# Where linear attention's outputs are gated, and when their gates are fetched, in a one-core hybrid layer

## The chip, the cores and the metric

The kernel runs on one core of a Trainium2 chip. The core has TensorE for matmuls (PE; its weight loads, PEld, overlap them), VectorE (DVE), ScalarE (ACT), GpSimd (POOL) and SyncE (SP); each works through its own instructions in order, and 16 transfer engines move data between memory and SBUF for the queues of SP, ACT and POOL. Matmuls accumulate in PSUM banks of 128 x 512 fp32. The metric is device time in microseconds (us) of one execution.

## The reference

One layer, 256 tokens, width 2048, fp32. From x come three groups of dilated attention (8 heads of 128), a gated linear attention (4 heads, 512 values each) and gates:

```
parts = split(x @ w_in)                       # 9 attention parts, gq, gk, gv, gr, g_low, m_a, m_b
ya = softmax-weighted sum of the 3 groups' outputs @ w_proj_a
o  = linear attention(gq, gk, gv, decay from g_low), per head
o  = o * rsqrt(mean(o * o) + eps) * gla_norm_g
yb = (o * silu(gr)) @ w_proj_b
y  = sigmoid(m_a) * ya + sigmoid(m_b) * yb
x  = layernorm(alpha * x + y @ w_out)
x  = layernorm(alpha * x + (silu(conv3(x @ w_gate)) * (x @ w_up)) @ w_down)
```

silu(gr) is gr * sigmoid(gr). What is called *gating* below is o * silu(gr), for each head h and each half t of the tokens (128 tokens x 512 values).

## The kernel before

Each fp32 weight piece (128 x 1024, 512 KB) is loaded by SP and split into two parts that PE multiplies at full rate: ACT copies the high part (`whi`, L137), DVE subtracts for the low part (`wlo`, L138). There are six buffers for high parts and four for low ones. PE then takes three matmuls for one product (high x high, low x high, high x low). So every weight passes ACT and DVE before PE, and what stands ahead of a split in ACT's or DVE's order delays it.

The stages, in PE's order:

- **First stage** (to about 838 us): tiles of q and k (`b16`, L237) alternate with units of seven products (`seven`, L318) for the values `v`, the linear attention's `gv`, `gr`, and the gates `m`. Their results are spilled to memory. Beside them run short steps: attention's (list `side`) and linear attention's (list `slow`: for each head fetch, decay, keys, scores, outputs, the last spilling o by L723). `pump` (L186) is called between steps; it takes one step of `slow` on every second call and one or more of `side` on each. A step may carry a mark and waits until the unit that passes this mark is done.
- **Plain gate chunks** (L788, 838 to 889 us; tiles `m_t`): the last quarter of the gates by plain products (`a_chunk`, L268). The projected attention outputs are fetched and split meanwhile (`ya_parts`, L780).
- Then the pool of early buffers is closed and one of late buffers is opened at the same place in SBUF (L796, L797). The first instruction that uses the late pool is POOL's memset of three buffers (L801).
- **yp** (L859): four chunks of ya @ w_proj_a. Each chunk fetches its two gates from memory on POOL's queue, takes their sigmoid (L855), and multiplies them with the product (L863). Beside yp run the four steps `gated_out` (L837): fetch gr and o of a head into the late pool, sigmoid (L843), two products (L844, L845), and turn the result by PE into PSUM banks (`transposed`, L805 and L814), from which ACT and DVE take its high and low part (L821, L822) as the operand `ob` of the next stage.
- **pb** (L869): four chunks of the gated outputs @ w_proj_b, times their gates, plus ya. Then w_out, the layer norm, and the feed-forward part (from 1135 us), which the change leaves alone.

ACT loads a table of functions when an instruction needs one that isn't loaded (`ACT_TABLE_LOAD`): exponential and logarithm stand in one, sigmoid in another.

The order on each engine is set by a scheduler that places the recorded instructions, so that it differs from the order of the code; buffers and the recorded dependences bound it.

Of the kernel before, what the change touches and what calls it, by code (L numbers as in the profile page):

```python
# [11 lines left out]
F32 = mybir.dt.float32  # L12
F32R = mybir.dt.float32r
AF = mybir.ActivationFunctionType
# [3 lines left out]
P = 128  # L18
S = 256
# [39 lines left out]
def hybrid_layer(ctx: ExitStack, tc: tile.TileContext, wp, xt, wgl, gw, par, relb, onehot, rows, xk, out):  # L59
# [53 lines left out]
    def fetch(name, d, make=None, by=None):  # L113
        b = (make or blk)(name)
        (by or nc.gpsimd).dma_start(b, d)
        return b
# [19 lines left out]
    def split(hi, lo, src):  # L136
        nc.scalar.activation(hi, src, AF.Copy)  # L137
        nc.vector.tensor_tensor(lo, src, hi.bitcast(F32), op=ALU.subtract)  # L138
# [485 lines left out]
    def gla(h):  # L624
# [153 lines left out]
    YA2 = [res("ya") for _ in range(2)]  # L778

    def ya_parts(h):  # L780
        def f():
            y = YA2[h // 4][:, h % 4]
            split(y[:, :S], y[:, S:], fetch("yaf", YA[h], tmp))
        return f

    side.extend(ya_parts(h) for h in range(NH))
    yop = lambda kc: YA2[kc // 4][:, kc % 4]
    for n in range(2):  # L788
        pss = a_chunk("m", xop, 16, AT["mb"] + 8 * n, 3)
        for t in range(2):  # L790
            c = blk("mc")
            nc.scalar.activation(c, pss[t], AF.Copy)
            M[1][2 + n][t] = spill("ms", c)
    drain()
    home[:] = "quarter", 12
    early.close()  # L796
    now[:] = ctx.enter_context(tc.tile_pool(name="late", bufs=1)), (17, 10, 1)  # L797
    gbufs = []
    for i in range(3):
        g = now[0].tile([P, S + 2], F32, name=f"gbuf{i}")  # L800
        nc.gpsimd.memset(g[:, 0:2], 0.0)  # L801
        gbufs.append(g)


    def transposed(name, n, halves_of_tokens, gain=None):  # L805

# [25 lines left out]
        return opnd  # L832


    OB = []

    def gated_out(h):  # L837
        def f():
            g = []
            for t in range(2):  # L840
                x, o = fetch("gr", GR[h][t]), fetch("o", O[h][t])
                sg = blk("sg")
                nc.scalar.activation(sg, x, AF.Sigmoid)  # L843
                nc.vector.tensor_tensor(sg, sg, x, op=ALU.mult)  # L844
                nc.vector.tensor_tensor(sg, sg, o, op=ALU.mult)  # L845
                g.append(sg)
            OB.extend(transposed("ob", h, g, P_NG))
        return f

    side.extend(gated_out(h) for h in range(GH))  # L850
    last_gate = []

    def gate(br, n, t):
        g = fetch("m", M[br][n][t])
        last_gate[:] = [nc.scalar.activation(g, g, AF.Sigmoid)]  # L855
        return g

    ya = []
    for n in range(4):  # L859
        g = [gate(0, n, t) for t in range(2)]  # L860
        pss = a_chunk("yp", yop, 8, AT["pa"] + 4 * n)
        for t in range(2):
            nc.vector.tensor_tensor(g[t], g[t], pss[t], op=ALU.mult)  # L863
        ya.append(g)
    drain()


    YT = []
    for n in range(4):  # L869
        g = [gate(1, n, t) for t in range(2)]  # L870
        pss = a_chunk("pb", by_pairs(OB), 16, AT["pb"] + 8 * n)
        for t in range(2):
            y = g[t]
            nc.vector.tensor_tensor(y, y, pss[t], op=ALU.mult)
            nc.vector.tensor_tensor(y, y, ya[n][t], op=ALU.add)
        side.append(lambda n=n, y=g: YT.extend(transposed("yt", n, y)))
    drain()

# [272 lines left out]
```

## Time and profile before

| | us |
|---|---|
| median of three runs (1877.98 to 1884.69) | 1882.73 |
| the profiled execution's own time | 1883.29 |
| its span, first to last instruction | 1881.6 |
| PE / DVE / ACT / POOL busy | 1835.3 / 1348.2 / 1037.2 / 153.1 |
| first stage and plain gate chunks end, yp begins | 889.15 |
| yp ends, pb begins | 945.93 |

The profile is of one execution. A row of a timeline reads: start, duration, engine, line, operation, written<-read tiles, shapes, and in brackets how long the engine was idle before and what ended that. A row of waits reads: engine, tile and line that waited, what it waited for; sum in us, times, longest. A row of windows: the stretch, its length, busy us and instructions of PE, PEld, DVE, ACT and POOL, the granted share of TensorE's clock, the busy share of the transfer engines, GB/s. A group's row ends with busy us, mean ns of one | idle us before them and what ended it.

### The profile page before, as it was taken

The page shows a single profiled execution, that of the slowest core. Times are in us where ns is not written, and L with a number is a line of the kernel's source. Part 1 is how long each engine was busy: PE and PEld are TensorE (multiplying, and loading weights), DVE is VectorE, ACT ScalarE, POOL GpSimd, SP SyncE. Part 2 cuts the span into 40 slices and gives each one's busy share as a digit, 9 for nine tenths or more (in the row PEclk, how much of TensorE's full clock was granted, in tenths as well). Part 3 has the DMA queues.
Part 4 walks back from the last instruction along what each step waited for, and adds up shares of the span by engine and source line. Part 5 has one row for each costly group of instructions (what it writes and reads, how often), then busy time and mean ns, then how long its engine had stood idle before and what let it go on. Part 6 is the DMA issues. An engine that isn't in the chain of part 4 may idle for free.

```text
span 1881.6 us, 25449 instructions
## 1 busy us (share of the span) xinstructions
PE 1835.3 (98%) x9270; PEld 1549.8 (82%) x9270; DVE 1348.2 (72%) x1613; ACT 1037.2 (55%) x1346; POOL 153.1 (8%) x241
## 2 busy tenths in 40 slices
PE   8999999999999999999899999999999999999997
PEld 6778778888888888888688877888888888888885
DVE  7889878888787978875755568666546666456667
ACT  6467556666766666654644446555335554345452
POOL 0011111101111111101300001000000000000001
PEclk9999999999999999999999999999999999999998
DMA  8478996978979798795876557555655566565651
GB/s 313 166 282 255 305 319 184 341 223 270 325 224 343 203 307 287 244 333 179 313 235 204 196 168 232 188 193 187 201 185 195 182 196 194 192 231 193 193 167 45
DMA packets 131849, 432.39 MB, mean 230 GB/s; under 512 B 15601, under 2 KB 25868, under 8 KB 131724
## 3 DMA queue, kind: packets, MB, share of 16 engines
q1 hardware_dynamic: 96764, 345.09, 52.5%
q0 software_dynamic: 21424, 73.53, 15.9%
q10 hardware_dynamic: 13536, 12.16, 2.1%
q8 instruction: 72, 1.18, 0.2%
q14 instruction: 53, 0.43, 0.1%
HBM read 372.97 MB, written 21.14 MB: 209 GB/s over the span
## 4 chain that ended last, share of the span: by engine, by line
PE 86%; DMA 4%; DVE 2%; issue 1%; ACT 1%; DVEq 0%; SPq 0%; ACTq 0%; POOLq 0%
PE qk L228 9%; PE fu L228 8%; PE fg L228 8%; PE fu L230 4%; PE qk L230 4%; PE fg L230 4%; PE wd_t L264 4%; PE wd_t L266 4%; PE wd_t L265 4%; DMA quarter<-in_wp 2%; PE pb_t L266 2%; PE pb_t L265 2%; PE pb_t L264 2%; PE wo_t L264 2%; PE wo_t L265 2%; PE wo_t L266 1%
## 5 line engine op out<-in xcount | busy, mean ns | idle before, releaser
L138 DVE TENSOR_TENSOR wlo<-quarter,whi 128x1024 fp32r<-128x1024 f32 x624 | 747.6, 1221 | 354.2 <-PE wd_t L265 84.2
L137 ACT ACTIVATE whi<-quarter 128x1024 fp32r<-128x1024 f32 x624 | 655.8, 1057 | 478.6 <-PE wd_t L266 95.9
L137 ACT ACTIVATE whi<-raw 128x1024 fp32r<-128x1024 f32 (+1 forms) x146 | 151.4, 1044 | 86.4 <-PE qk L228 38.1
L228 PE MATMUL qk<-x,whi 128*128 128x512 f32 x768 | 195.2, 403 | 0.0
L138 DVE TENSOR_TENSOR wlo<-raw,whi 128x1024 fp32r<-128x1024 f32 (+1 forms) x146 | 173.3, 1205 | 30.6 <-ACT whi L137 10.8
L228 PEld LDWEIGHTS qk<-x,whi 128*128 128x128 f32 x768 | 143.6, 190 | 30.5 <-issue 1.2
L228 PE MATMUL fu<-x,whi 128*128 128x512 f32 x688 | 164.1, 391 | 0.0
L228 PE MATMUL fg<-x,whi 128*128 128x512 f32 x672 | 160.2, 390 | 0.0
L228 PEld LDWEIGHTS fu<-x,whi 128*128 128x128 f32 x688 | 126.4, 188 | 24.5
L228 PEld LDWEIGHTS fg<-x,whi 128*128 128x128 f32 x672 | 123.7, 188 | 24.0
L264 PE MATMUL wd_t<-whi,h 128*128 128x512 f32 x352 | 137.0, 389 | 0.0
L265 PE MATMUL wd_t<-wlo,h 128*128 128x512 f32 x352 | 137.0, 389 | 0.0
L266 PE MATMUL wd_t<-whi,h 128*128 128x512 f32 x352 | 136.9, 389 | 0.0
L345 DVE TENSOR_TENSOR quarter<-quarter,quarter 128x1024 f32<-128x1024 f32 x88 | 104.4, 1217 | 0.4
L230 PEld LDWEIGHTS qk<-x,wlo 128*128 128x128 f32 x768 | 98.6, 191 | 3.8
L230 PE MATMUL qk<-x,wlo 128*128 128x256 f32 x768 | 99.6, 283 | 0.0
L230 PEld LDWEIGHTS fu<-x,wlo 128*128 128x128 f32 x688 | 88.2, 191 | 3.4
L230 PE MATMUL fu<-x,wlo 128*128 128x256 f32 x688 | 89.2, 283 | 0.0
L348 POOL DMA_DIRECT2D quarter<-quarter x72 | 62.9, 873 | 321.7 <-DMA quarter<-in_wp 175.0
L230 PEld LDWEIGHTS fg<-x,wlo 128*128 128x128 f32 x672 | 86.2, 191 | 3.3
L230 PE MATMUL fg<-x,wlo 128*128 128x256 f32 x672 | 87.2, 283 | 0.0
L266 PEld LDWEIGHTS wd_t<-whi,h 128*128 128x128 f32 x352 | 66.1, 188 | 13.8
(316 smaller groups left out, 2765.7 us busy)
## 6 DMA issues: line engine op xcount, KB each, us to landing
quarter<-in_wp SPq DMA_DIRECT2D x504, 512.0 KB, 4.5
raw<-in_wp SPq DMA_DIRECT2D x142, 512.0 KB, 6.7
quarter<-quarter POOLq DMA_DIRECT2D x72, 512.0 KB, 9.5
row<-in_rows POOLq DMA_DIRECT2D x16, 256.0 KB, 5.1
sp<-c POOLq DMA_DIRECT2D x14, 256.0 KB, 9.2
bias<-bvd ACTq DMA_DIRECT2D x32, 96.0 KB, 5.4
v<-vs ACTq DMA_DIRECT2D x24, 128.0 KB, 4.5
m<-sp POOLq DMA_DIRECT2D x12, 256.0 KB, 4.8
```

The costliest lines, as they stand in the source:

```text
L137: nc.scalar.activation(hi, src, AF.Copy)
L138: nc.vector.tensor_tensor(lo, src, hi.bitcast(F32), op=ALU.subtract)
L228: nc.tensor.matmul(ps, parts(kc)[0], opnd(kc), start=(kc == 0), stop=False)
L230: nc.tensor.matmul(ps[:, S:], parts(kc)[1], opnd(kc)[:, :S], start=False, stop=(kc == nk - 1))
L264: nc.tensor.matmul(ps, xh, hi, start=first, stop=False)
L265: nc.tensor.matmul(ps, xh, lo, start=False, stop=False)
L266: nc.tensor.matmul(ps, xl, hi, start=False, stop=last)
L345: tt(a, a, b, op=ALU.add)
L348: nc.gpsimd.dma_start(a, b, accum_op=ALU.add)
```

## The change

Fetching gr and o, sigmoid and both products leave yp and become steps of `slow` in the first stage, behind linear attention's own steps and behind the mark "gr"; once that mark is passed, `pump` takes a step of `slow` on every call. The fetches go out on ACT's queue; the result is spilled (`og`) by POOL. The turned operands of heads 0 and 1 are made in the plain gate chunks, those of heads 2 and 3 in yp; each turn's operand is fetched in an earlier step. Fetch and split of the attention outputs are two steps now, the last two heads' in yp. The gates of yp and pb are fetched one chunk ahead, and their sigmoid is recorded behind the chunk's matmuls.

```diff
     def pump(n=1):
         turns[0] += 1
-        if turns[0] % 2 == 0:
+        if turns[0] % 2 == 0 or "gr" in passed:
             following(slow)
...
+    def gated(h):
+        st = []
+        def get():
+            for t in range(2):
+                st.append([fetch("gr", GR[h][t], by=nc.scalar), fetch("o", O[h][t], by=nc.scalar)])
+        def mul():
+            sgs = [blk("sg") for _ in range(2)]
+            for sg, (x, o) in zip(sgs, st):
+                nc.scalar.activation(sg, x, AF.Sigmoid)
+                nc.vector.tensor_tensor(x, x, o, op=ALU.mult)
+            for t, (sg, (x, o)) in enumerate(zip(sgs, st)):
+                nc.vector.tensor_tensor(sg, sg, x, op=ALU.mult)
+                O[h][t] = spill("og", sg)
+        return get, mul
...
         for stages in gla_stages:
             slow.extend(stages)
+        for h in range(GH):
+            get, mul = gated(h)
+            slow.extend([("gr", get), lambda: None, mul])
...
-        yield from by_unit("gr", 2, lambda u: to(GR, u))
+        yield from by_unit("gr", 2, lambda u: to(GR, u), "gr")
...
-    side.extend(ya_parts(h) for h in range(NH))
+    def ob_get(h):
+        def f():
+            got[h] = [fetch("og", O[h][t]) for t in range(2)]
+        return f
+    def ob_turn(h):
+        def f():
+            OB[2 * h : 2 * h + 2] = transposed("ob", h, got[h], P_NG)
+        return f
...
+    slow.extend([
+        lambda: (ob_get(0)(), ya_get(0, 1)),
+        lambda: ya_get(2, 3),
+        lambda: (ya_split(0, 1), ob_turn(0)()),
+        lambda: (ya_split(2, 3), ob_get(1)()),
+        lambda: ya_get(4, 5),
+        lambda: ob_turn(1)(),
+        lambda: ya_split(4, 5),
+    ])
     for n in range(2):
         pss = a_chunk("m", xop, 16, AT["mb"] + 8 * n, 3)
...
-    side.extend(gated_out(h) for h in range(GH))
+    def gates_ahead():
+        ahead = None
+        for br in range(2):
+            for n in range(4):
+                new = [fetch("m", M[br][n][t]) for t in range(2)]
+                if ahead is None and not (br or n):
+                    ya_get(6, 7)
+                    for h in (2, 3):
+                        ob_get(h)()
+                else:
+                    yield ahead
+                ahead = new
+        yield ahead
+    ahead_of = gates_ahead()
+    def gated_by(g, pss):
+        for x in g:
+            last_gate[:] = [nc.scalar.activation(x, x, AF.Sigmoid)]
+        for x, ps in zip(g, pss):
+            nc.vector.tensor_tensor(x, x, ps, op=ALU.mult)
+    side.extend([lambda: ya_split(6, 7), ob_turn(2), lambda: None, ob_turn(3)])
     for n in range(4):
-        g = [gate(0, n, t) for t in range(2)]
+        g = next(ahead_of)
         pss = a_chunk("yp", yop, 8, AT["pa"] + 4 * n)
-        for t in range(2):
-            nc.vector.tensor_tensor(g[t], g[t], pss[t], op=ALU.mult)
+        gated_by(g, pss)
```

(pb changes in the same way; `transposed` itself stays as it is.)

Three places in the engines' orders. The first is PE in yp, where it changes from chunk 0 (`yp_t_1069`/`1070` before, `yp_t_1117`/`1118` now) to chunk 1 (`yp_t_1095`; now `yp_t_1128`/`1129`). `pt` are the turns, read from a head's gated output (`sg` before, `og` now). Before:

```order
L264 MATMUL yp_t_1070_8162<-whi_8254,ya_7727 128x512
L265 MATMUL yp_t_1070_8162<-wlo_8255,ya_7727 128x512
L266 MATMUL yp_t_1070_8162<-whi_8254,ya_7727 128x512
L264 MATMUL yp_t_1095_8313<-whi_8317,ya_7726 128x512
L814 MATMUL pt_8216<-ident,sg_8203 128x128
L814 MATMUL pt_8225<-ident,sg_8203 128x128
L265 MATMUL yp_t_1095_8313<-wlo_8318,ya_7726 128x512
```

Now:

```order
L264 MATMUL yp_t_1118_8294<-whi_8355,ya_7807 128x512
L265 MATMUL yp_t_1118_8294<-wlo_8356,ya_7807 128x512
L266 MATMUL yp_t_1118_8294<-whi_8355,ya_7807 128x512
L807 MATMUL pt_8372<-ident,og_8281 128x128
L807 MATMUL pt_8372<-ident,og_8283 128x128
...
L807 MATMUL pt_8381<-ident,og_8283 128x128
L264 MATMUL yp_t_1129_8399<-whi_8402,ya_7806 128x512
```

Before, the turn of head 0 stood behind the 48 matmuls of chunk 0 and one of chunk 1; now that of head 2 stands behind the 48 and three of chunk 1, both halves together.

The second place is POOL's queue where the late pool opens: `ms` are the spills of the last plain gate chunk, `m` the gates of yp's first chunk. Before:

```order
L110 DMA ms_8119<-mc_8117 128x512
L110 DMA ms_8123<-mc_8121 128x512
L801 MEMSET gbuf_8149 128x2
...
L115 DMA m_8155<-sp_6111 128x512
L115 DMA m_8158<-sp_6234 128x512
L115 DMA gr_8199<-sp_4591 128x512
L115 DMA o_8201<-os_4305 128x512
L115 DMA gr_8207<-sp_4691 128x512
L115 DMA o_8209<-os_4317 128x512
```

Now:

```order
L110 DMA ms_8257<-mc_8255 128x512
L110 DMA ms_8261<-mc_8259 128x512
L878 MEMSET gbuf_8267 128x2
...
L115 DMA m_8273<-sp_6161 128x512
L115 DMA m_8275<-sp_6279 128x512
L115 DMA yaf_8277<-yas_7860 128x256
L115 DMA yaf_8279<-yas_8217 128x256
L115 DMA og_8281<-og_6849 128x512
L115 DMA og_8283<-og_6852 128x512
```

The two gates still come first behind the memset; the place of gr and o of head 0 is taken by two attention outputs of half the size and then the gated outputs of head 2.

The third place is the first stage. On DVE, before the first split (`wlo`) of the product `mB` of the second gate unit (`quarter` are the unit's weights, which are added to each other), there stood before:

```order
L658 TENSOR_TENSOR gz_6467<-gc_6236 128x512
L345 TENSOR_TENSOR quarter_6303<-quarter_6303,quarter_6474 128x1024
L345 TENSOR_TENSOR quarter_6305<-quarter_6305,quarter_6476 128x1024
L138 TENSOR_TENSOR wlo_6488<-quarter_6299,whi_6487 128x1024
```

Now (rows between left out):

```order
L740 TENSOR_TENSOR gr_6355<-gr_6355,o_6357 128x512
L740 TENSOR_TENSOR gr_6359<-gr_6359,o_6361 128x512
L742 TENSOR_TENSOR sg_6473<-sg_6473,gr_6355 128x512
L742 TENSOR_TENSOR sg_6474<-sg_6474,gr_6359 128x512
...
L345 TENSOR_TENSOR quarter_6375<-quarter_6375,quarter_6559 128x1024
L138 TENSOR_TENSOR wlo_6571<-quarter_6369,whi_6570 128x1024
```

The four products of head 0 have come in, one operation (L658) of the last linear attention head has gone to an earlier place. On ACT, some 25 us later, where an attention head's two exponentials stand (L476), before:

```order
L476 ACTIVATE s_825_6403,l_6650<-s_825_6403,nm_6648 128x384
L476 ACTIVATE s_826_6404,l_6657<-s_826_6404,nm_6655 128x768
L137 ACTIVATE whi_6730<-quarter_6474 128x1024
L137 ACTIVATE whi_6740<-quarter_6476 128x1024
L137 ACTIVATE whi_6765<-raw_6763 128x1024
```

Now, from the second of these exponentials on; ahead of it, between the two, stand a table load, the two sigmoids of head 1, and ahead of the first a further table load:

```order
L476 ACT_TABLE_LOAD
L476 ACTIVATE s_854_6486,l_6746<-s_854_6486,nm_6744 128x768
L137 ACTIVATE whi_6809<-quarter_6555 128x1024
L137 ACTIVATE whi_6819<-quarter_6557 128x1024
L115 DMA gr_6729<-sp_5355 128x512
...
L115 DMA o_6735<-os_5798 128x512
L256 ACTIVATE pa_6796<-qk_6763 128x256
L137 ACTIVATE whi_6829<-quarter_6559 128x1024
L739 ACT_TABLE_LOAD
L739 ACTIVATE sg_6842<-gr_6729 128x512
L739 ACTIVATE sg_6843<-gr_6733 128x512
L137 ACTIVATE whi_6866<-raw_6864 128x1024
```

The fetches of head 2 and its sigmoids have come between the splits, with one copy (`pa`) and one split between fetch and use. In all ACT's order holds eleven table loads where it held five.

More of the change, by code (lines that the diff above doesn't have):

```diff
@@ L775, in hybrid_layer @@
             done += 1
[L778 to L784, printed above, removed]
-    side.extend(ya_parts(h) for h in range(NH))
-    yop = lambda kc: YA2[kc // 4][:, kc % 4]
-    for n in range(2):
-        pss = a_chunk("m", xop, 16, AT["mb"] + 8 * n, 3)
-        for t in range(2):
[L791 to L802, printed above, removed]
     def transposed(name, n, halves_of_tokens, gain=None):
@@ L832, in by_pairs @@
         return opnd
-    OB = []
-    def gated_out(h):
+    OB = [None] * 8
+    got = {}
+    def ob_get(h):
         def f():
[L839 to L847, printed above, removed]
-        return f
@@ L850, in hybrid_layer, with ya_get @@
-    side.extend(gated_out(h) for h in range(GH))
-    last_gate = []
[L853 to L856, printed above, removed]
+            got[h] = [fetch("og", O[h][t]) for t in range(2)]
+        return f
+    def ob_turn(h):
+        def f():
+            OB[2 * h : 2 * h + 2] = transposed("ob", h, got[h], P_NG)
+        return f
+    YA2 = [res("ya") for _ in range(2)]
+    yaf = {}
+    def ya_get(*hs):
+        for h in hs:
+            yaf[h] = fetch("yaf", YA[h], tmp)
@@ new lines, in ya_split @@
+    def ya_split(*hs):
+        for h in hs:
+            y = YA2[h // 4][:, h % 4]
+            split(y[:, :S], y[:, S:], yaf[h])
+    slow.extend([
[7 more added lines that the diff above has]
+    ])
+    yop = lambda kc: YA2[kc // 4][:, kc % 4]
+    for n in range(2):
+        pss = a_chunk("m", xop, 16, AT["mb"] + 8 * n, 3)
+        for t in range(2):
+            c = blk("mc")
+            nc.scalar.activation(c, pss[t], AF.Copy)
+            M[1][2 + n][t] = spill("ms", c)
@@ new lines, in hybrid_layer @@
+    drain()
+    home[:] = "quarter", 12
+    early.close()
+    now[:] = ctx.enter_context(tc.tile_pool(name="late", bufs=1)), (17, 10, 1)
+    gbufs = []
+    for i in range(3):
+        g = now[0].tile([P, S + 2], F32, name=f"gbuf{i}")
+        nc.gpsimd.memset(g[:, 0:2], 0.0)
+        gbufs.append(g)
+    last_gate = []
+    def gates_ahead():
[11 more added lines that the diff above has]
+        yield ahead
```

8 lines of the change are left out of this document (3 added, 5 removed).

## The prediction

> **What bounds the kernel.** The page first: share of the engines, then the chain that ended last.
>
> ```profile
> PE 1835.3 (98%) x9270; PEld 1549.8 (82%) x9270; DVE 1348.2 (72%) x1613; ACT 1037.2 (55%) x1346; POOL 153.1 (8%) x241
> PE 86%; DMA 4%; DVE 2%; issue 1%; ACT 1%; DVEq 0%; SPq 0%; ACTq 0%; POOLq 0%
> ```
>
> TensorE is busy for 98% of the span and carries 86% of the chain. Whatever the change moves between the other engines is worth only what TensorE stops waiting, and it leaves TensorE's own work alone: the 32 turns of gated outputs stand elsewhere in its order, but none is added. So the second view is the list of waits, for PE.
>
> ```profile
> PE pt L814 <- issue: 7.7, 1, 7.7
> ...
> PE ps L465 <- DVE s L467: 4.2, 3, 2.9
> ```
>
> The longest wait of the whole execution is one of 7.7 us before a turn (L814), in the chunks that this change rewrites. The third view is PE's timeline around it, with the granted clock of the stretches behind it and of one after the 2.9 us wait of the second row.
>
> ```profile
> 900.03 0.39 PE L264 MATMUL yp_t<-whi,ya 128*128 128x512 f32 x1
> 908.14 0.66 PE L814 MATMUL pt<-ident,sg 128*128 128x128 f32 x2 [7.72 <-issue]
> 908.45 0.78 PE L265 MATMUL yp_t<-wlo,ya 128*128 128x512 f32 x1
> ...
> 911.57 0.39 PE L266 MATMUL yp_t<-whi,ya 128*128 128x512 f32 x1
> ```
>
> ```profile
> 281.00:286.80 5.80, 5.80 (x14) 4.56 (x15) 3.55 (x8) 3.55 (x7) 0.48 (x1) 0.50 0.97 391
> ...
> 904.80:908.10 3.30, 0.00 (x0) 0.00 (x0) 1.45 (x3) 2.48 (x4) 2.09 (x4) 0.50 1.03 417
> 908.20:911.40 3.20, 3.20 (x9) 2.62 (x10) 2.77 (x4) 0.80 (x2) 0.61 (x2) 0.50 1.01 408
> ```
>
> PE stops at 900.4 and takes up work at 908.14; the clock is at half from about 904.8 to 911.4, so the 3.1 us from 908.45 to 911.57 do 1.6 us of work. Wait and clock cost 7.7 + 1.5 = 9.2 us, 0.5% of the span. That is all there is to win here. The 2.9 us wait was followed by about 6 us at half clock too: a shorter wait starts again earlier inside the slow stretch and pays more of it.
>
> **What the wait consists of.** The timelines of PE, ACT and POOL, and four transfers, the two spills and two of the fetches (size, then us from issue to landing):
>
> ```profile
> 889.15 0.39 PE L264 MATMUL yp_t<-whi,ya 128*128 128x512 f32 x1
> ```
>
> ```profile
> 888.89 1.07 ACT L137 ACTIVATE ya<-yaf 128x256 fp32r<-128x256 f32 x3 [1.15 <-DMA yaf<-yas]
> 889.87 0.58 ACT L792 ACTIVATE mc<-m_t 128x512 f32<-128x512 f32 x1
> ...
> 890.65 0.59 ACT L792 ACTIVATE mc<-m_t 128x512 f32<-128x512 f32 x1
> ...
> 902.36 1.28 ACT L855 ACT_TABLE_LOAD   x1 [6.16 <-issue]
> ```
>
> ```profile
> 891.54 0.54 POOL L110 DMA_DIRECT2D ms<-mc  x1 [0.25 <-ACT mc L792]
> 896.90 0.17 POOL L801 MEMSET gbuf<- 128x2 f32 x3 [4.82 <-DMA quarter<-in_wp]
> 897.41 0.54 POOL L115 DMA_DIRECT2D m<-sp  x1 [0.34 <-issue]
> ...
> 899.73 0.54 POOL L115 DMA_DIRECT2D gr<-sp  x1
> ```
>
> ```profile
> ms<-mc POOLq DMA_DIRECT2D x1, 256.0 KB, 3.5
> ```
>
> ```profile
> ms<-mc POOLq DMA_DIRECT2D x1, 256.0 KB, 5.1
> ```
>
> ```profile
> m<-sp POOLq DMA_DIRECT2D x1, 256.0 KB, 4.7
> ```
>
> ```profile
> gr<-sp POOLq DMA_DIRECT2D x1, 256.0 KB, 7.3
> ```
>
> Let E be the end of the plain gate chunks, 889.15, where the first matmul of yp starts. Both results are copied out (to 891.2), the second spill goes out at 891.54 and lands 5.1 us later at 896.6 (the first spill took 3.5); only then is the early pool closed, and the memset at 896.90 opens the late one (the row's named releaser had long been done; the spill is what ends there). Every fetch into the late pool stands behind that: the first lands at 897.41 + 4.7, and only then ACT loads the sigmoid's table. PE has 49 matmuls of yp (11.1 us) to do meanwhile, and then stands at a turn.
>
> **The change there.** By the order of the changed kernel PE has 51 matmuls of yp, 51 x 0.227 = 11.6 us, and then the turn of head 2. Sigmoid, two products and the table load no longer stand ahead of that turn, but the gated output that it turns is again fetched into the late pool, as the fifth and sixth transfer after the same memset. So the barrier stays and only what followed it shrinks. In times from E: the three splits ahead of the first copy are gone, so the second copy ends at about E+1.1 to 1.4 (E+2.1 before); spill 3.5 to 5.1; memset and first issue E+5.5 to E+7.2 (E+8.3 before). The fifth transfer of 256 KB landed at 899.73 + 7.3 = 907.0, 9.6 us after the first issue; the two transfers of 128 KB among the six now make sixth place about equal to it: 9.6 to 10.3. The turn's operands are there at E+15.1 to E+17.5, against PE's arrival at E+11.6: a wait of 3.5 to 5.9 us, say 4.6. It begins as before, so the half clock begins as before too, and PE comes back with 4.5 to 6 us of it to run, which costs some 2.6 us. Together 7.2 against 9.2: a gain of **2.0 us**. Its ends: nothing, if the landings are as late as the latest above; and with the shortest of each (copies 1.1, spill 3.5, issue of six 3.2, landing 4.7) a wait of 0.9 us and no slow clock, a gain of 8.
>
> **What the change adds to the first stage.** The gating of four heads now lies between about 687 and 750 us: 16 fetches on ACT's queue, 8 sigmoids, 16 products on DVE, 8 spills, and six more table loads (the order shows eleven where there were five), because sigmoids now stand between exponentials. Prices and the state of that stretch (a window; then DVE, PE; fetches of the same size on ACT's queue; ACT, PE; groups):
>
> ```profile
> 700.00:710.00 10.00, 10.00 (x47) 8.31 (x46) 10.00 (x12) 8.06 (x10) 0.00 (x0) 1.00 0.07 16
> ```
>
> ```profile
> 703.48 4.62 DVE L138 TENSOR_TENSOR wlo<-quarter,whi 128x1024 fp32r<-128x1024 f32 x4
> ```
>
> ```profile
> 705.18 0.62 PE L332 MATMUL mB<-wlo,comb 128*128 128x512 f32 x2
> ```
>
> ```profile
> gq<-gkqs ACTq DMA_DIRECT2D x8, 256.0 KB, 8.3
> gv<-sp ACTq DMA_DIRECT2D x8, 256.0 KB, 10.8
> ...
> gc<-gcs ACTq DMA_DIRECT2D x4, 256.0 KB, 6.7
> ```
>
> ```profile
> 719.40 0.33 ACTq L453 DMA_DIRECT2D bias<-bvd  x1
> ...
> 724.21 1.06 ACT L137 ACTIVATE whi<-raw 128x1024 fp32r<-128x1024 f32 x1 [0.55 <-ACT whi L137]
> ```
>
> ```profile
> 733.40 3.91 PE L228 MATMUL qk<-x,whi 128*128 128x512 f32 x16
> ```
>
> ```profile
> L972 ACT ACT_TABLE_LOAD x1 | 1.3, 1283 | 0.0
> ```
>
> ```profile
> L843 ACT ACTIVATE sg<-gr 128x512 f32<-128x512 f32 x8 | 5.0, 624 | 0.8 <-DMA gr<-sp 0.8
> ```
>
> ```profile
> L844 DVE TENSOR_TENSOR sg<-sg,gr 128x512 f32<-128x512 f32 x8 | 5.5, 688 | 8.1 <-ACT sg L843 8.1
> ```
>
> *Head 0, on DVE.* DVE has no free time from 700 to 710, and the first of four splits at 703.48 ends at 704.7, when PE takes it at 705.18: half a microsecond to spare. In the new order head 0's four products (4 x 0.69 = 2.75 us) stand ahead of that split, and one operation of 0.68 us of the linear attention's last head has gone from there. Without any wait PE loses 2.75 - 0.68 - 0.5 = 1.6 us. The products also wait for the sigmoid, and that for its fetch, issued two splits and a copy out of PSUM before it, by PE's pace there an estimated 6 us; with the 8.3 us of the fetch rows about 1.2 us more, with 10.8 some 4 more, with 6.7 none. I take 2.4 (1.6 to 5.6).
>
> *Head 2, on ACT.* The order has the four fetches, one copy and one split, then table load and sigmoids: the fetch is used some 4 us after its issue and takes 6.7 to 10.8, so ACT stands still for about 4 us, and the splits of the following weights stand behind it. The piece next in line was made at 725.3 and taken at 733.40, 8.1 us to spare. Ahead of it come four table loads (5.1), four sigmoids (2.5), four issues (1.3) and that wait (4): 13 us, less an estimated 2 us in which ACT idled there (0.55 in its row) and the 2.4 that PE has already lost: 8.5 to 9 us. I take 2.0, more than the 0.5 left over, because DVE stands behind ACT; bounds 0 and 5 (with 10.8 us of landing). Heads 1 and 3 have their fetch long done by then, and I cost them at nothing; whi buffers six pieces ahead are their cover.
>
> [...]
>
> **The plain gate chunks.** Heads 0 and 1 are turned there; 16 of the 32 turns leave yp, which is PE's time moved and not changed. Their two banks are wanted again after 10 and 11 matmuls (2.3 and 2.5 us) by the last attention head, while four evictions on ACT, each followed by one on DVE, empty them:
>
> ```profile
> L821 ACT ACTIVATE ob<-pt,prm 128x256 fp32r<-128x256 f32 x16 | 6.8, 468 | 1.7 <-PE pt L814 1.4 <-DVE ob L822 0.3
> ```
>
> Four times 0.47 with a DVE step behind is 2.4 us, more if a split lies between. I take **0.8 us** (0 to 3). Gates fetched a chunk ahead I cost at nothing: their sigmoids already ran far ahead of need, hidden under yp's 44 us of matmuls; without that cover each pair would cost its 1.2 us.
>
> **The sum.** The profiled execution took 1883.29 us, 0.56 above the median of 1882.73, inside the spread of the three runs. 1883.29 - 2.0 + 2.4 + 2.0 + 0.8 = **1886.5 us**, 0.2% above the median.
>
> **Rivals.** *The wait goes.* If six transfers land within 5 us of the memset, PE meets its operands on time: minus 8, and with 1.6 us lost on DVE 1876.9. For it: the first landing of 4.7. Against: the fifth's 9.6 after the first issue, with the transfer engines full (1.03 and 1.01 in the two windows of the slow clock). 8%. *ACT blocked in the first stage.* Slower: where a fetch on ACT's queue takes 10 us or more, ACT's queue stands at the sigmoid of heads 0 and 2 until the weights run out; 5.6 + 5 us, and as each wait is then longer than the 2.9 after which the clock was seen at half, about 3 us more for one of them: 1883.3 - 2 + 10.6 + 3 + 0.8 = 1895.7; from about 9 us of landing it is over the bound of 0.3%. For it: the 10.8 us row. Against: the 6.7 us row. 36%, which includes the cases between the forecast and that price. *The change does nothing there*, since the first stage has room for all of it: 1883.3 - 2 = 1881.3; against it stands DVE's full window. This counts within the forecast's case, no difference.
>
> **Chances.** About 0.3%, 5.6 us, is what a measurement of this kernel tells from no change. No difference (the forecast and the last rival) 56%, slower by more 36%, faster by more 8%. Range: from 1878 (most of the wait gone, little lost) to 1895 (most of the second rival).
>
> **What would show it.** In the changed kernel's waits: a wait of PE at the turn of head 2, 3.5 to 5.9 us, about 11.6 us behind the start of yp, with half clock behind it; idle time of ACT before the new table loads; PE waiting for a split of DVE near 705 and for ACT or DVE near 735; a short wait of PE for a bank in the plain gate chunks. The forecast is wrong if the wait at the turn is under 1 us, or if the first stage's PE waits sum to under 1 or over 9 us.

## The result, and the profile after

The changed kernel took 1904.23 us in the median of six runs (1899.46 to 1910.25), where the kernel before, run beside it, took 1883.04 (1877.98 to 1885.63). The ratio is 1.0113 with a 95% interval of 1.009 to 1.0136: it is about 1.1% slower. The forecast was 1886.5 us with a range of 1878 to 1895, so the time lies outside the range, on the side of the rival *ACT blocked in the first stage*. The profiled execution took 1899.46 us.

The page of the changed kernel gives the share of the engines; PE does the same work as before (1835.3 us then) in a longer span:

```profile
PE 1836.0 (97%) x9270; PEld 1548.5 (82%) x9270; DVE 1347.8 (71%) x1613; ACT 1041.8 (55%) x1352; POOL 154.0 (8%) x241
```

The first matmul of each stage, in PE's timeline, cuts the two profiled executions into stretches (us):

| stretch | before | after | difference |
|---|---|---|---|
| first stage up to the gate units (`mA`) | 603.8 | 599.6 | -4.2 |
| gate units and attention, up to `m_t` | 234.8 | 254.4 | **+19.6** |
| plain gate chunks, up to `yp_t` | 50.6 | 57.2 | **+6.6** (1.8 of it the 16 turns that moved here) |
| yp, up to `pb_t` | 56.8 | 51.3 | **-5.4** (1.8 of it the turns that left) |
| all behind it | 935.7 | 935.3 | -0.4 |

The first row is not the change. Three kernels below leave the first stage as it was before, and the stretch from the first `v` unit to the first `gv` unit, which holds this difference, took 242.6, 244.5 and 244.9 us in them, 244.3 in the changed kernel, and 248.4 only in the one profiled execution of before. Without the turns that merely moved, the change costs 19.6 + 4.8 - 3.6 = 20.8 us.

PE's waits in the changed kernel (engine, tile and line, releaser: sum, times, longest) name the three places:

```profile
PE qk L228 <- ACT whi L137: 11.1, 3, 8.2
PE ps L465 <- DVE s L467: 8.8, 5, 2.6
...
PE yp_t L264 <- ACT ya L137: 4.1, 1, 4.1
```

**The gate units.** The longest wait of before, 7.7 us at a turn in yp, is gone, and one of 8.2 us stands in the first stage: PE waits for a high part that ACT makes. The timelines of PE and of ACT there show why (ACTq are the transfers that ACT issues):

```profile
736.93 0.27 PE L486 MATMUL ppt<-ident,s 128*128 128x128 f32 x1
...
745.44 0.80 PE L228 MATMUL qk<-x,whi 128*128 128x512 f32 x1 [8.23 <-ACT whi L137]
```

```profile
726.15 0.34 ACTq L115 DMA_DIRECT2D gr<-sp  x1
...
727.47 1.30 ACTq L115 DMA_DIRECT2D gr<-sp  x1
...
734.97 1.28 ACT L739 ACT_TABLE_LOAD   x1 [2.30 <-DMA gr<-sp]
736.26 0.63 ACT L739 ACTIVATE sg<-gr 128x512 f32<-128x512 f32 x1
743.81 0.63 ACT L739 ACTIVATE sg<-gr 128x512 f32<-128x512 f32 x1 [6.91 <-DMA gr<-sp]
744.34 1.99 ACT L137 ACTIVATE whi<-raw 128x1024 fp32r<-128x1024 f32 x2
```

The second `gr` of head 2 is issued at 727.47 and used at 743.81, 16.3 us later. ACT stands 2.3 us ahead of the table load and 6.9 ahead of the second sigmoid, and the split that PE needs at 737 is the next instruction on ACT's queue, at 744.34. Some 2.7 us into the wait, which begins at 737.2, the granted clock falls to 0.50. Windows of the changed kernel (stretch, length, busy us of PE, PEld, DVE, ACT and POOL, granted clock, share of the transfer engines, GB/s):

```profile
737.00:739.90 2.90, 0.20 (x2) 0.00 (x0) 0.44 (x1) 0.00 (x0) 0.00 (x0) 1.00 1.05 289
739.90:750.20 10.30, 4.76 (x11) 3.80 (x12) 3.59 (x6) 6.39 (x8) 1.62 (x3) 0.50 0.88 333
```

Of the 10.3 us at half clock 4.8 lie behind the wait, and cost 2.4 us of work: 8.2 + 2.4 = 10.6 us from this one place. DVE stood for the other operand of the gating too, 18 us in five waits:

```profile
DVE gr L740 <- DMA o<-os: 18.0, 5, 6.7
```

Transfers on POOL's queue were slow too, and they had been before. First the transfers issued between 725 and 745 us in the profile of *before* (size, us to landing), then those of the changed kernel:

```profile
sp<-c POOLq DMA_DIRECT2D x1, 256.0 KB, 13.0
sp<-s POOLq DMA_DIRECT2D x1, 256.0 KB, 8.5
bias<-bvd ACTq DMA_DIRECT2D x2, 96.0 KB, 10.7
```

```profile
og<-sg POOLq DMA_DIRECT2D x2, 256.0 KB, 17.1
sp<-c POOLq DMA_DIRECT2D x1, 256.0 KB, 18.2
```

So the trace of before held a part of the answer: in just this stretch 96 KB on ACT's queue took 10.7 us, and of two transfers of 256 KB on POOL's queue one took 13.0 and one 8.5. Why the second `gr` took 16.3 is not shown.

**The plain gate chunks.** ACT, DVE and PE of the changed kernel, around the second wait of the list (2.3 us of it here):

```profile
865.78 1.06 ACT L137 ACTIVATE whi<-raw 128x1024 fp32r<-128x1024 f32 x1 [1.60 <-DMA raw<-in_wp]
869.16 0.42 ACT L137 ACTIVATE ya<-yaf 128x256 fp32r<-128x256 f32 x1 [2.32 <-DMA yaf<-yas]
...
869.49 1.04 ACT L137 ACTIVATE whi<-raw 128x1024 fp32r<-128x1024 f32 x1
```

```profile
869.61 0.42 DVE L138 TENSOR_TENSOR ya<-yaf,ya 128x256 fp32r<-128x256 f32 x1 [3.40 <-ACT ya L137]
869.96 1.22 DVE L138 TENSOR_TENSOR wlo<-raw,whi 128x1024 fp32r<-128x1024 f32 x1
871.09 0.28 DVE L467 SCALAR_TENSOR_TENSOR s<-ps,bias 128x128 f32<-128x128 f32 x1
```

```profile
871.43 0.70 PE L465 MATMUL ps<-qk 128*128 128x256 f32 x2 [2.26 <-DVE s L467]
```

The split of an attention output waits 2.3 us for its fetch; DVE stands for it, a weight split is next, and only then comes the step that frees a bank of the attention head's scores. It is the same pattern as above. PE's waits in this stretch sum to 4.1 us: this one, one of 1.0 for a turn's bank and one of 0.8 for a copy of ACT; before the change it had none.

**yp.** POOL and PE of the changed kernel:

```profile
911.49 1.22 POOL L110 DMA_DIRECT2D ms<-mc  x2 [4.49 <-ACT mc L869]
917.27 0.17 POOL L878 MEMSET gbuf<- 128x2 f32 x3 [4.56 <-DMA ms<-mc]
...
918.85 1.06 POOL L115 DMA_DIRECT2D yaf<-yas  x2
```

```profile
919.69 0.39 PE L266 MATMUL yp_t<-whi,ya 128*128 128x512 f32 x1
924.22 0.80 PE L264 MATMUL yp_t<-whi,ya 128*128 128x512 f32 x1 [4.14 <-ACT ya L137]
```

The barrier of the two pools is as forecast: last spill, memset, then fetches. But PE does not stop at the turn of head 2. It stops sooner, inside chunk 0, whose last pieces read the attention outputs of heads 6 and 7, which the change now fetches into the late pool too.

### The profile page after: what moved, and what is told of

Its sections match the earlier page's. It is cut to its first block, busy times and chain, and to the rows that moved or that the text cites. A ratio compares the mean times of both kernels' runs of the same rounds, so it can differ in the third digit from the quotient of the medians.

```text
span 1897.7 us, 25455 instructions
## 1 busy us (share of the span) xinstructions
PE 1836.0 (97%) x9270; PEld 1548.5 (82%) x9270; DVE 1347.8 (71%) x1613; ACT 1041.8 (55%) x1352; POOL 154.0 (8%) x241
## 4 chain that ended last, share of the span: by engine, by line
PE 51%; issue 3%; DVE 1%; DMA 1%; ACT 1%; POOL 0%; POOLq 0%; DVEq 0%; ACTq 0%
PE fu L228 8%; PE fg L228 8%; PE fu L230 4%; PE fg L230 4%; PE wd_t L264 4%; PE wd_t L266 4%; PE wd_t L265 4%; PE wo_t L265 2%; PE wo_t L264 2%; PE pb_t L266 2%; PE pb_t L265 2%; PE pb_t L264 2%; PE wo_t L266 2%; PE yp_t L264 1%; PE yp_t L265 1%
```

## The experiments

Each kernel's one profiled execution was cut into the same stretches; ratios are against the kernel before, run beside it. In the expectations "from the second gate's units to the plain gate chunks" means the stretch from `mA` to `m_t`.

| kernel | `mA` to `m_t` | `m_t` to yp | yp | ratio, 95% interval |
|---|---|---|---|---|
| before | 234.8 | 50.6 | 56.8 | 1 |
| the changed kernel | 254.4 | 57.2 | 51.3 | 1.0113 (1.009 to 1.0136) |
| fetch farther ahead, all heads | 242.8 | 59.8 | 52.5 | 1.0078 (1.0061 to 1.0096) |
| the same, head 2 alone | 244.0 | 58.9 | 51.6 | 1.0063 (1.0038 to 1.0088) |
| fetch farther ahead, on POOL's queue | 241.0 | 62.0 | 52.3 | 1.0047 (1.0032 to 1.0062) |
| no fetches | 241.6 | 57.2 | 52.5 | 1.0041 (1.0025 to 1.0056) |
| fetches alone | 238.8 | 57.8 | 51.5 | 1.0057 (1.0035 to 1.008) |
| copy in place of sigmoid | 250.1 | 58.0 | 51.4 | 1.0098 (1.0065 to 1.0132) |
| gating alone moved | 254.4 | 50.5 | 57.6 | 1.0094 (1.0069 to 1.0118) |
| turns back in yp | 252.3 | 57.6 | 53.4 | 1.011 (1.0071 to 1.0148) |
| attention outputs early | 252.2 | 58.1 | 53.6 | 1.0124 (1.0106 to 1.0143) |
| before, turns late | 235.0 | 50.5 | 54.1 | 0.9994 (0.998 to 1.0008) |
| before, turns spread | 234.9 | 50.6 | 48.1 | 1.0011 (1.0 to 1.0022) |
| before, turns spread and gates ahead | 235.1 | 50.6 | 47.1 | 0.9966 (0.9952 to 0.9981) |

### Which part of the change carries the loss: the gating alone

The kernel before, with `gated`, its steps and `pump`'s new condition taken over, and `gated_out` cut to a fetch and the turns:

```diff
     def gated_out(h):
         def f():
-            g = []
...
+            g = [fetch("og", O[h][t]) for t in range(2)]
             OB.extend(transposed("ob", h, g, P_NG))
```

> The kernel before, with the gating alone moved into the first stage; turns, attention outputs and gates stay where they were, and the turns in yp read the fetched gated outputs. Theory (the first stage carries the loss): the stretch from the start of the second gate's units to the plain gate chunks is 17 to 21 us longer than before, the plain gate chunks stay within 1 us of before, the wait before the first turn in yp falls from 7.7 us to 3 to 5 us: 1894 to 1900 in all. Rival (the turns in the plain gate chunks and the fetch of attention outputs carry it): at most 6 us over the time before.

The stretch of the gate units is as long as in the whole change (254.4), and the plain gate chunks are as before (50.5). So the moved gating carries the 19.6 us, and nothing of the 6.6. The time, 1900.4 us, was just above the band expected, because one point of the theory missed: the wait before the first turn did not shorten.

```profile
924.17 0.66 PE L835 MATMUL pt<-ident,og 128*128 128x128 f32 x2 [8.45 <-DMA quarter<-in_wp]
```

It grew from 7.7 to 8.4 us, though sigmoid and products no longer stand ahead of the turn. (The releaser named is a weight's transfer; the turn reads `og`, whose fetches POOL issued from 917.4 on, behind its memset at 915.8.) What PE waited for in yp was the barrier and the landings, not the gating.

### Is it the landing: the fetch farther ahead

In the changed kernel:

```diff
-            slow.extend([("gr", get), lambda: None, mul])
+            slow.extend([("gr", get), *[lambda: None] * 4, mul])
```

> The changed kernel with one edit: three more idle steps between a head's fetch and its sigmoid, so that 13 to 25 instructions of ScalarE lie between the fetch of heads 0 to 2 and its use, where 4 to 20 lay. Table loads (11), sigmoids and products stay. Theory (ScalarE stands still at a sigmoid whose fetch hasn't landed, with the weights' splits behind it): ScalarE's idle time ahead of the gating's sigmoids and table loads (2.3 + 6.9 us at head 2) goes, the 8.2 us wait of TensorE before the qk tile and the 10.2 us at half clock behind it go too, and the time falls by 10 to 14 us, to 1886 to 1890. Rival (it is ScalarE's and VectorE's added work and the table loads, not the landing): the waits move with the work, and the time stays within 4 us of the changed kernel's.

The 8.2 us wait is gone, no idle time of ACT stands ahead of a gating sigmoid or its table load, and the stretch is 11.6 us shorter. The time was 1895.73 us, 8.5 below the changed kernel's, short of the 10 to 14 expected, as the plain gate chunks took back 2.6. And ACT still stood 7.2 us once, in another way:

```profile
756.06 0.33 ACTq L115 DMA_DIRECT2D gr<-sp  x1
...
757.28 0.33 ACTq L115 DMA_DIRECT2D o<-os  x1
...
759.36 0.33 ACTq L115 DMA_DIRECT2D gr<-sp  x1
...
762.32 0.33 ACTq L115 DMA_DIRECT2D o<-os  x1
...
762.75 2.01 ACT L137 ACTIVATE whi<-raw 128x1024 fp32r<-128x1024 f32 x2 [7.16 <-DMA gr<-sp]
```

Four issues of 0.33 us are 1.2 to 3 us apart, and the next split comes behind the last: here ACT stands at the *issue* of a fetch, which itself waits for an earlier transfer (which one is seen in the kernel with the fetches alone, below).

With the further idle steps for head 2 alone (`(4 if h == 2 else 1)`):

> The changed kernel with the three further idle steps between fetch and sigmoid for head 2 alone; heads 0, 1 and 3 as in the changed kernel, the same 11 table loads. With the far fetch for all heads the stretch from the second gate's units to the plain gate chunks fell from 254.4 to 242.8 us. Theory (one landing, that of head 2's second gr, 16 us after its issue, with the 8.2 us wait and the 10.2 us at half clock behind it): head 2 alone brings most of this, a stretch of 241 to 246 us, and ScalarE's 6.9 us idle time before the second sigmoid is gone. Rival (each head's fetch costs its part, a quarter each): 250 us or more.

One head's fetch brings 10.4 of the 11.6 us. The rival, a quarter for each head, falls.

### What remains: arithmetic or transfers

In the changed kernel, `get` without its fetches:

```diff
-                st.append([fetch("gr", GR[h][t], by=nc.scalar), fetch("o", O[h][t], by=nc.scalar)])
+                st.append([blk("gr"), blk("o")])
+                for x in st[t]:
+                    nc.gpsimd.memset(x, 1.0)
```

> The changed kernel with the fetches of gr and o in the first stage left out: the gating works on tiles of ones that GpSimd sets long before, so this leaves out the real gate and output values; table loads (11), sigmoids, products and spills stay. From the start of the second gate's units to the plain gate chunks the kernel before took 234.8 us, the changed one 254.4, the one with the far fetch 242.8. Theory (what the far fetch left, 8 us, is the added work of ScalarE and VectorE in a stretch where VectorE has no free time): that stretch takes 240 to 244 us. Rival (the 8 us are the added 4 MB of fetches, as the transfer engines are full there): 235 to 238 us.

241.6 us, inside the theory's band: the gating's arithmetic and spills cost 6.8 us with no fetch to wait for. But it is not all arithmetic, as the theory had it. ACT stands 8.0 us here too, until a *spill* has landed, that of a gated output:

```profile
744.18 0.49 ACT L491 ACTIVATE pT<-ppt 128x384 f32<-128x384 f32 x1 [8.00 <-DMA og<-sg]
```

POOL had issued it at 726.96, 17.1 us before. `pT` and `sg` are taken from one pool of buffers (`blk`), so the copy presumably waits for the buffer. PE's waits for the unit whose weights ACT splits next follow right behind, 0.8 and 1.8 us. In the opposite kernel `mul` does nothing:

> The changed kernel with the gating's arithmetic and spills left out of the first stage and nothing in their place, so the outputs pass ungated; the 16 fetches on ScalarE's queue are issued at the same steps and nothing waits for them. Theory (ScalarE's and VectorE's work and the wait for the landing): the stretch from the second gate's units to the plain gate chunks is within 2 us of the 234.8 of before. Rival (the transfers delay the weights): 238 us or more.

Here the theory missed and the rival came true, 238.8 us, but not because a split waited for its own weight. ACT and PE of this kernel:

```profile
753.45 0.49 ACT L491 ACTIVATE pT<-ppt 128x384 f32<-128x384 f32 x1 [9.25 <-DMA gr<-sp]
```

```profile
754.93 1.61 PE L332 MATMUL mE<-whi,x 128*128 128x512 f32 x4 [2.52 <-ACT whi L137]
```

Nobody reads the fetched tiles, and yet ACT stands 9.3 us between two activations, in which four fetches are issued one by one. The trace also records the semaphores (counters by which a transfer reports its landing): each of the four goes out, 747.35 to 753.07, within 0.1 us of the landing of a weight's transfer that SP had issued 11 to 16 us earlier and that reports by the same semaphore as the fetch. So the four fetches on ACT's queue held up ACT without being used. The last kernel tests this: the far fetch, issued on POOL's queue (the fetches without `by=nc.scalar`).

> The far-fetch kernel with one edit: the 16 fetches of gr and o are issued on GpSimd's queue and not on ScalarE's; steps, 11 table loads, sigmoids, products and spills stay. In the far-fetch kernel ScalarE stood 7.2 us at the fetches of head 2 themselves (four issues 1.2 to 3 us apart, the weights' splits behind them), and in the kernel with the fetches alone 9.3 us. Theory (an issue on ScalarE's queue waits for earlier transfers, and ScalarE with it): without them the stretch from the gate units' start to the plain gate chunks falls from 242.8 to 238 to 241 us, and no idle time of ScalarE there is ended by a landing of gr. Rival (the adding-up transfers of weights, which GpSimd issues in order behind the fetches, come late instead): 243 us or more, with waits of TensorE for products of the gate units.

No idle time of ACT in this stretch ends with a landing of `gr` any more, and the stretch fell from 242.8 to 241.0 us, the upper end of the expectation. The 1.8 us are one profile against one, and the plain gate chunks took 62.0, 2.2 more; the gain of this step is small. But the stretch is now as short as without any fetch (241.6): issued early and from POOL, the fetches add nothing to it that one profile could show.

### Is it the table switches

In the changed kernel, without the sigmoid of the gates:

```diff
-                nc.scalar.activation(sg, x, AF.Sigmoid)
+                nc.scalar.activation(sg, x, AF.Copy)
```

> The changed kernel with a copy in place of the sigmoid of gr in the gating; this leaves the sigmoid out of that part of the computation, so that no table is switched in the first stage (5 table loads in all, as before the change, where the changed kernel has 11). Fetches, products and spills stay. Theory (the wait for the fetch): the wait of TensorE at head 2 stays, as ScalarE stands at the copy instead of the sigmoid; six loads of 1.28 us fewer, of which only those at heads 1 and 2 can show: 2 to 5 us faster than the changed kernel. Rival (the table switches block ScalarE): 12 us or more faster, down to the time before the change.

The stretch is 4.3 us shorter, the profiled execution 4.1 us, the median 6.7 (2 to 5 was expected). The wait at head 2 stays, with nothing to switch:

```profile
PE qk L228 <- ACT whi L137: 6.9, 2, 6.3
```

So the loads are a part of the cost, and not what blocks ACT.

### The plain gate chunks: turns or attention outputs

In the changed kernel, the turns of heads 0 and 1 back in yp (their two steps and fetches leave the list of the plain gate chunks):

```diff
-    side.extend([lambda: ya_split(6, 7), ob_turn(2), lambda: None, ob_turn(3)])
+    side.extend([lambda: ya_split(6, 7), lambda: None, ob_turn(0), lambda: None, ob_turn(1), ob_turn(2), lambda: None, ob_turn(3)])
```

> The changed kernel with the turns of heads 0 and 1 put back into yp, behind 72 and 120 of its matmuls; the early fetches and splits of the attention outputs in the plain gate chunks stay as the change has them, gating stays in the first stage. The plain gate chunks took 50.6 us before and 57.2 in the changed kernel, 1.8 of the 6.6 more being the 16 turns. Theory (the turns' banks and the evictions on ScalarE and VectorE hold up the last attention heads): the plain gate chunks take 50.5 to 52 us. Rival (the order of fetches and splits of the attention outputs in steps of two heads does it): 54 us or more.

My theory fell: without any turn the plain gate chunks take 57.6 us. ACT stands at the split of an attention output as in the changed kernel, and PE's wait for the attention head's bank is 4.2 us (the second row is of its waits):

```profile
868.61 0.42 ACT L137 ACTIVATE ya<-yaf 128x256 fp32r<-128x256 f32 x1 [2.67 <-DMA yaf<-yas]
```

```profile
PE ps L465 <- DVE s L467: 8.5, 4, 4.2
```

The granted clock behind that wait, the same view as in the windows above:

```profile
871.30:878.10 6.80, 5.68 (x13) 4.47 (x14) 2.72 (x4) 1.28 (x2) 0.00 (x0) 0.50 0.45 140
```

PE comes back at 872.42, so 5.7 us at half clock lie behind the wait and cost 2.8: with 4.2 they are the 7.0 us by which this stretch is longer than before. Since moving the gating alone left this stretch at 50.5, the new order of the attention outputs' steps is the cause, which puts a split that waits for its fetch ahead of a running attention head.

### What stands in yp

The changed kernel with heads 6 and 7 fetched and split ahead of yp:

```diff
+    side.extend([lambda: ya_get(6, 7), lambda: ya_split(6, 7)])
...
-                    ya_get(6, 7)
...
-    side.extend([lambda: ya_split(6, 7), ob_turn(2), lambda: None, ob_turn(3)])
+    side.extend([lambda: None, ob_turn(2), lambda: None, ob_turn(3)])
```

> The changed kernel with the last two attention outputs fetched and split ahead of yp, as before the change; so no matmul of chunk 0 of yp waits for a transfer into the late pool, and TensorE reaches the turn of head 2 first, behind 48 matmuls. Theory (the barrier of the pools and six landings, as forecast): a wait of 3.5 to 6 us at that turn in place of the changed kernel's 4.1 us for ya, at half clock behind it; yp about as long as the changed kernel's 51.4 us. Rival (the landings were short and only the attention outputs were late): no wait over 1.5 us at the turn, yp 46 to 48 us.

```profile
PE pt L807 <- DMA og<-og: 5.9, 1, 5.9
```

The wait for `ya` is gone, and the wait at the turn of head 2 that the prediction described appears, 5.9 us, at the upper end of its 3.5 to 5.9. It had been hidden behind the wait for `ya`, which comes first in PE's order. yp takes 53.6 us, where the changed kernel took 51.3.

### Can the wait of before go without moving the gating

Three idle steps ahead of `gated_out` in the kernel before:

> The kernel before with one edit: three idle steps ahead of the gated outputs in yp, so that TensorE reaches the first turn behind 96 matmuls of yp and not behind 49; nothing else is moved, gating and its fetches stay in yp. Theory (the wait before was only a matter of the turn's place: the barrier of the two pools and the landings take about 19 us from the start of yp, and 96 matmuls last 22): the 7.7 us wait and the half clock behind it go, the time falls by 7 to 9 us, to 1874 to 1876. Rival (the barrier holds up something else that TensorE needs, or the turns then crowd at the end of yp): a wait of 3 us or more appears elsewhere in yp or at the start of pb, and the time falls by less than 4.

The theory missed, and the time is the rival's. The 7.7 us wait is gone, but a new one of 2.7 us for a turn's bank stands in yp (`pt` for DVE's `ob`), as the turns now stand close together, and with 1880.18 us the time is that of before. Spreading them,

```diff
+    side.extend([idle] * 3 + [gated_out(0), idle, gated_out(1), idle, gated_out(2)])
...
     drain()
+    side.append(gated_out(3))
```

> The kernel before with the gated outputs' steps in yp set later and further apart: the turns come behind 96, 144, 192 matmuls of yp and 24 of pb; nothing is moved into the first stage. Before, the late turn alone (all four close together behind 96) shortened yp from 56.8 to 54.1 us, with a new wait of 2.9 us for a turn's bank. Theory (that wait came from the turns standing close together, so that each turn's evictions stood behind the next head's products): no wait over 1 us in yp and no half clock there; yp and pb together 139 to 141 us where before took 146.5, and 1874 to 1877 us in all. Rival (VectorE, with the same products and evictions, is late wherever the turns stand): waits of 3 us or more in yp and pb, and no change of over 3 us.

shortened yp to 48.1 us, but lengthened pb from 89.8 to 101.1. No change for the better again (ratio 1.0011), as the rival had it, but not for its reason, a late DVE: a wait of 7.7 us came back, now in pb, where ACT stood with a turn's eviction queued behind gates that were fetched late. The change's "gates a chunk ahead" bears on just that. So the last kernel of this line takes this one part from the change, and splits gating and turn into steps of their own:

```diff
...
+    side.extend([idle, idle, mul(0), mul(1), turn(0), mul(2), turn(1), mul(3)])
     ya = []
     for n in range(4):
-        g = [gate(0, n, t) for t in range(2)]
+        g = next(ahead_of)
         pss = a_chunk("yp", yop, 8, AT["pa"] + 4 * n)
-        for t in range(2):
-            nc.vector.tensor_tensor(g[t], g[t], pss[t], op=ALU.mult)
+        gated_by(g, pss)
         ya.append(g)
     drain()
+    side.extend([turn(2), turn(3)])
...
```

> The kernel before with yp alone rewritten: gates fetched a chunk ahead with their sigmoid behind the chunk, as in the change; gating stays in yp, in steps of its own, and each head is turned a step or more behind its gating; the turns come behind 120 and 168 matmuls of yp and 24 and 48 of pb. The first stage and the plain gate chunks are those of before. In the spread version before this one, TensorE waited 7.7 us in pb for a bank, as ScalarE stood with the evictions behind gates whose fetch was late. Theory (with the gates a chunk ahead nothing that TensorE needs in yp waits for a landing into the late pool): no wait over 1.5 us in yp and pb, no half clock there, yp and pb together 138 to 141 us where before took 146.5; 1872 to 1876 us in all, 0.3 to 0.4% under before. Rival (some buffer or bank comes late again wherever the steps stand, since VectorE and ScalarE carry the same work beside yp): a wait of 3 us or more there, and a time within 3 us of before.

1874.31 us against 1881.46 (ratio 0.9966, 0.9952 to 0.9981): about 0.3% **faster than before**, and so faster than the changed kernel too. One wait of 1.9 us for a bank remains in pb, with half clock behind it, so the expectation of none over 1.5 and no half clock failed by a little, and yp and pb together took 142.5 us where 138 to 141 was expected and 146.5 was before.

## Why the prediction was wrong, step by step

- **Head 2 on ACT, costed at 2.0 us (0 to 5), is the step that failed.** The mechanism was written down (ACT stands at the sigmoid, the splits behind it, 8.1 us of spare time), and only its size was off. I priced the landing at 6.7 to 10.8 us, from medians over the whole first stage. The first `gr` of the head kept to that (issued at 726.15, waited for until 734.97, 8.8 us); the second took 16.3, and 15.7 in the kernel with the copy. PE's wait was 8.2 us and its slow clock cost 2.4, 10.6 us where the bound was 5, and moving this one fetch gave back 10.4. Rows of the very stretch, in the trace of before, had up to 13.0 us for 256 KB, still less than it took.
- **Head 0 on DVE, 2.4 us (1.6 to 5.6)**, was about right, at its low end: PE waited 0.6 us near 709 at the low part that was named, and 1.0 us near 701 for a step of an attention head on DVE.
- **Heads 1 and 3, at nothing**, were not free: ACT stood 3.6 us at a sigmoid of head 3, and PE waited 1.9 us, to 767.5, for a high part. The fetches' issues were costed at 0.33 us each; in the kernel with the fetches alone ACT stood 9.3 us at four of them. Arithmetic and spills cost 6.8 us without any fetch, where the prediction had 1.6 to 2.4 for head 0 and spare time for the rest. It had no term for a spill's landing, behind which 2.5 of them lie.
- **The table loads.** The price of 1.28 us stood. ACT of the changed kernel:

```profile
723.68 1.16 ACT L739 ACTIVATE sg<-gr 128x512 f32<-128x512 f32 x2
724.85 1.28 ACT L476 ACT_TABLE_LOAD   x1
726.15 0.94 ACT L476 ACTIVATE s<-s,nm 128x768 f32<-128x768 f32 x1
```

The load starts as the sigmoids end, and the exponential starts as the load ends. Without all six this stretch was 4.3 us shorter, less than their own 7.7.
- **The plain gate chunks, 0.8 us (0 to 3), cost 4.8.** The bank wait that was named is there, 1.0 us; what was overlooked is that the attention outputs' splits moved too, to where their fetch is late. That is shown for this one wait, 2.3 us here and 4.2 with the turns back in yp. With the bank's 1.0 and a wait of 0.8 for a copy of ACT, whose cause is open, it makes 4.1 of the 4.8.
- **yp, -2.0 (-8 to 0), gave -3.6.** The barrier was right and the wait at the turn was right in size, as the run with early attention outputs shows. But in the changed kernel PE met another tile first, whose fetch I had quoted in POOL's order and not followed to its reader: a wait of 4.1 us in place of 3.5 to 5.9. PE did not wait at the turn at all, which the prediction had named as a sign of being wrong, so that the yp term came out near is in part luck.
- **The sum.** 1886.5 had +3.2 us in all; the stretches give +20.8, less 4.2 in the first row of the table and 0.4 behind. From the gate units to the plain gate chunks PE's waits sum to 16.9 us, where before had 1.1; over 9 was the prediction's other sign of being wrong. The rival *ACT blocked* had the right cause and 1895.7 us; it fell short in the same landing, and in the plain gate chunks.

## What to carry to other kernels

A transfer's landing time is read in the stretch where the transfer will run and for all queues there, not from a median over a stage: here it was 16 us against medians of 7 to 11, and up to 13 in that stretch. An engine that prepares what the bottleneck needs next should neither use a transfer near its landing nor issue one that may have to wait, nor take over a buffer whose spill is still under way: here ACT stood 6.9 us for the first in the changed kernel, 9.3 for the second in the one with the fetches alone, and 8.0 for the third in the one with no fetches. And every tile that is moved into a later buffer pool is followed to its first reader. Where a wait stands behind a barrier, moving the reader back can do more than moving the work: here later turns with gates fetched ahead took 0.3% off the time, where the moved gating added to it.

## What was not expected of the hardware

The time at half clock behind a wait did not follow from the wait's length. In the changed kernel the 8.2 us brought a slow stretch of 10.3 us, and the 4.1 us in yp one of 3.5 (second row); the 2.3 us of wait in the plain gate chunks brought none (first row). But 1.9 us in pb, in the kernel with turns spread and gates ahead, brought the clock to 0.77 over 7.5 us, an estimated 3.4 us at half by these two numbers (second fence; in the 3.4 us ahead of it, its first row, PE was busy for 1.5).

```profile
868.00:880.00 12.00, 9.16 (x44) 6.98 (x42) 5.72 (x9) 4.93 (x8) 0.00 (x0) 1.00 0.80 273
...
924.20:927.70 3.50, 3.48 (x8) 2.81 (x9) 0.76 (x2) 1.74 (x3) 1.70 (x4) 0.51 1.01 400
```

```profile
945.50:948.90 3.40, 1.47 (x12) 1.14 (x11) 2.65 (x5) 3.21 (x8) 0.00 (x0) 1.00 0.96 383
...
947.50:955.00 7.50, 7.25 (x29) 6.01 (x30) 5.74 (x9) 5.84 (x10) 1.06 (x2) 0.77 0.86 312
```

The stretches at half clock came in few lengths here. Those of the changed kernel, the end of the span left out, lasted 3.4 us (from 61.0, 101.7, 279.2 and 924.3 us), 10.2 (from 740.0) and 6.8 (from 1146.2); those of before lasted 6.8 us all five times (from 61.6, 102.6, 280.1, 904.7 and 1130.0). Two waits of like length, 4.1 us in yp of the changed kernel and 4.2 in the kernel with the turns back in yp, went with stretches of 3.4 and 6.8 us. What sets the length is not shown.
